# Splitting later weights beside the first MLP: own buffers, and each half chunk requested one step before its split

## Chip, cores, metric

The kernel runs on one core of one Trainium2 chip. The metric is the device time of one execution in microseconds, as the median of several runs. One further execution was taken with the hardware profiler; all rows below are from it.

## The reference

Two transformer layers of width 1024 over 1024 tokens, all in float32. Layer 0 mixes an mLSTM with a block-sparse attention, layer 1 is a sparse latent attention. Behind each mixer stand a LayerNorm, an MLP and a gated per-layer embedding:

```python
h = _layer_norm(DN_ALPHA * h + y, ln1_g[i], ln1_b[i])
u = jnp.square(jax.nn.relu(h @ mlp_w1[i])) @ mlp_w2[i]
h = _layer_norm(DN_ALPHA * h + u, ln2_g[i], ln2_b[i])
h = h + jax.nn.sigmoid(h @ ple_gate_w[i]) * (p[i] @ ple_w[i])
```

`mlp_w1` is 1024 x 4096 and `mlp_w2` 4096 x 1024 for each layer.

## The kernel before, in words

A float32 product is made of three reduced-precision ones: each operand is split into a high part (ScalarE copies it into the reduced type) and a low part (VectorE subtracts the high part), and `mm3` (L159) issues high x high, high x low and low x high, at L164, L167 and L168.

Weights that are used once are loaded into a `wraw` buffer and split there (`wload`, L103; L108 loads, L116 copies, L123 subtracts). Weights of layer 1's mixer that are used later, and more than once or in a hurry, are split ahead of time: `presplit` (L126) takes each [128, up to 1024] weight of `names1` (L884, 22 weights) in half chunks of at most 512 columns, 44 pieces in all. A piece takes two tiles, loads (through L83), copies (L137), subtracts in place (L138) and stores both parts to DRAM (through L86). `presplit` is a generator; `mlp` (L891) takes one step of it after every second output block (L926), in layer 0 alone.

The MLP goes in eight chunks of 512 hidden columns. The first half of a chunk makes the hidden columns: eight PSUM groups of 24 matmuls, each emptied by L907 (ScalarE, relu into a `w2` tile, L906), L908 (VectorE, square) and a split. The second half multiplies them by `mlp_w2`: sixteen PSUM groups of 12 matmuls, each added into H by VectorE (L916 in the first chunk, L918 in later ones). The PSUM tag for both has two banks. The `w2` tag has six buffers in this phase (L261, L482); `presplit` took its tiles from it too.

`tail` (L850) stands before the MLP in the same phase, with the same pools: the output projection with `e_wo`, the residual x loaded into `w2` tiles (L858), summed by L867, LayerNorm (L221) and transposes (L212). Its second half of `e_wo` goes through L116 and L123 as `wu`.

The order on each engine is not written out. A planner (L1652) simulates the program when it is built: each engine takes the instruction that stands earliest in the program among those that are ready and have a buffer, and that order is then fixed, engine by engine. SyncE issues all transfers, in order; an instruction waits for its operands, and whatever stands behind it on its engine waits as well. Buffers of one tag are given out in the order of the program.

Of the kernel before, what the change touches and what calls it, by code (L numbers as in the profile page):

```python
# [8 lines left out]
F32 = mybir.dt.float32  # L9
F32R = mybir.dt.float32r  # L10
BF16 = mybir.dt.bfloat16
I32 = mybir.dt.int32
AF = mybir.ActivationFunctionType
# [4 lines left out]
P = 128  # L18
# [29 lines left out]
class Kern:  # L48
# [77 lines left out]
    def presplit(self, names):  # L126

        nc = self.nc
        for key, src in names:
            n = src.shape[1]  # L130
            self.wd[key] = d = self.dram([P, 2, 1024], F32, "wd")
            for a in range(0, n, 512):
                b = min(a + 512, n)
                lo, hi = (self.w2(dt=F32R)[:, :b - a] for _ in range(2))
                raw = lo.bitcast(F32)
                self.load(raw, src[:, a:b])
                nc.scalar.activation(hi, raw, AF.Copy)  # L137
                nc.vector.tensor_sub(lo, raw, hi.bitcast(F32))  # L138
                self.store(d[:, 0, a:b], hi.bitcast(F32))
                self.store(d[:, 1, a:b], lo.bitcast(F32))  # L140
                yield

    def wget(self, key, n=1024, after=None, into=None):

# [1511 lines left out]
```

## Time and profile before

| | |
|---|---|
| median of three runs | 3027.05 us (3018.58 to 3027.65) |
| the profiled execution | 3019.71 us, span 3018.0 us |
| TensorE busy | 2901.9 us, 96% of the span |
| VectorE, ScalarE busy | 1645.1 us, 1108.4 us |
| granted TensorE clock, mean | 0.987 of full |
| first MLP, second MLP | 719.3 us, 704.5 us |

A row of stages gives, for a stretch of the span, the busy time of each engine with its count of instructions, the granted clock and the DMA engines' share. A row of waits names who waited, for whom, how long in total, how often and the longest. The chain of waits follows the work that ended last back from its end. Both MLPs consist of the same matmuls, so they can be laid side by side.

### The profile page before, as it was taken

To read this page: it belongs to the slowest core of one execution; us is meant where nothing else is said; L and a number is where in the kernel's file an instruction comes from. 1 tells how busy PE (TensorE), PEld (TensorE's weight loads), DVE (VectorE), ACT (ScalarE), POOL (GpSimd) and SP (SyncE) were. 2 spreads that over 40 slices of the span, in tenths; PEclk is the share of its full clock that TensorE was granted. 3 is DMA by queue.
4 is the path that set the end of the run, shared out by engine and by line. 5 is a ranking of instruction groups with operands and counts; after the bars stand their busy time and mean duration, and the time that the engine had idled before them with its cause. 6 is when DMAs were issued, how large, how long until landed. Compare 5 with 4: busy or idle time off the path is not lost.

```text
span 3018.0 us, 39426 instructions
## 1 busy us (share of the span) xinstructions
PE 2901.9 (96%) x14583; PEld 2437.8 (81%) x14583; DVE 1645.1 (55%) x3852; ACT 1108.4 (37%) x2136; POOL 444.8 (15%) x505
## 2 busy tenths in 40 slices
PE   9999999989999999999999897999899999999999
PEld 8888788878787787888887676889788888888887
DVE  3587677765433344334636999975453333333372
ACT  3356654643222222222323668654231111222131
POOL 0254221213000000000412220211120000000032
PEclk9999999999999999999999998999999999999999
DMA  5863544342332334211232347643501111111122
GB/s 198 256 237 121 187 140 152 121 147 101 120 100 87 121 126 139 85 50 49 98 134 79 126 148 252 241 148 131 192 29 56 42 56 42 56 42 56 42 84 84
DMA packets 161552, 352.85 MB, mean 117 GB/s; under 512 B 16976, under 2 KB 68560, under 8 KB 156624
## 3 DMA queue, kind: packets, MB, share of 16 engines
q1 hardware_dynamic: 161360, 350.34, 34.9%
q8 instruction: 115, 1.88, 0.3%
q14 instruction: 77, 0.63, 0.1%
HBM read 242.21 MB, written 108.07 MB: 116 GB/s over the span
## 4 chain that ended last, share of the span: by engine, by line
PE 79%; DVE 9%; DMA 6%; ACT 3%; issue 2%; SPq 0%; POOL 0%; POOLq 0%; ACTq 0%; DVEq 0%
PE psmm L164 21%; PE psmm L167 21%; PE psmm L168 21%; PE psx L823 2%; PE psx L813 2%; PE pss L784 2%; PE psx L212 1%; PE psx L1544 1%; DVE PT L96 1%; PE pss L164 1%; PE pss L167 1%; PE pss L168 1%; DMA qn<-stg 1%; DMA w<-o_wqn 1%; DMA w<-o_wcq 1%
## 5 line engine op out<-in xcount | busy, mean ns | idle before, releaser
L164 PE MATMUL psmm<-wsp,hid 128*128 128x512 f32 x1024 | 400.8, 391 | 12.0 <-DVE H L918 8.0
L168 PE MATMUL psmm<-wsp,hid 128*128 128x512 f32 x1024 | 399.2, 390 | 0.0
L167 PE MATMUL psmm<-h1T,wsp 128*128 128x512 f32 x1024 | 399.0, 390 | 0.2
L167 PE MATMUL psmm<-wsp,hid 128*128 128x512 f32 x1024 | 399.0, 390 | 0.0
L164 PE MATMUL psmm<-h1T,wsp 128*128 128x512 f32 x1024 | 398.2, 390 | 0.6 <-ACT h1T L95 0.6
L168 PE MATMUL psmm<-h1T,wsp 128*128 128x512 f32 x1024 | 398.2, 389 | 0.0
L116 ACT ACTIVATE wsp<-wraw 128x1024 fp32r<-128x1024 f32 (+1 forms) x173 | 182.1, 1053 | 512.2 <-PE psmm L168 477.1
L918 DVE TENSOR_TENSOR H<-psmm,H 128x512 f32<-128x512 f32 x224 | 154.0, 688 | 242.2 <-PE psmm L168 241.6
L908 DVE SCALAR_TENSOR_TENSOR w<-psmm,w 128x512 f32<-128x512 f32 x128 | 88.5, 692 | 340.9 <-ACT w L907 340.9
L123 DVE TENSOR_TENSOR wsp<-wraw,wsp 128x1024 fp32r<-128x1024 f32 (+1 forms) x155 | 192.2, 1240 | 132.6 <-ACT wsp L116 132.0
L201 POOL TENSOR_TENSOR brs<-pw,mhalf 128x1 f32<-128x1 f32 x32 | 25.6, 799 | 1471.3 <-DVE pw L200 1471.3
L164 PEld LDWEIGHTS psmm<-wsp,hid 128*128 128x128 f32 x1024 | 192.6, 188 | 55.5 <-DVE H L918 10.7
L168 PEld LDWEIGHTS psmm<-wsp,hid 128*128 128x128 f32 x1024 | 192.6, 188 | 40.4
L164 PEld LDWEIGHTS psmm<-h1T,wsp 128*128 128x128 f32 x1024 | 192.1, 188 | 40.8 <-ACT h1T L95 1.1
L167 PEld LDWEIGHTS psmm<-h1T,wsp 128*128 128x128 f32 x1024 | 192.2, 188 | 40.2 <-DVE h1T L96 0.8
L167 PEld LDWEIGHTS psmm<-wsp,hid 128*128 128x128 f32 x1024 | 192.7, 188 | 39.4
L168 PEld LDWEIGHTS psmm<-h1T,wsp 128*128 128x128 f32 x1024 | 192.3, 188 | 39.8
L907 ACT ACTIVATE w<-psmm 128x512 f32<-128x512 f32 x128 | 76.6, 598 | 395.4 <-PE psmm L168 395.4
L95 ACT ACTIVATE PT<-psx 128x512 fp32r<-128x512 f32 (+4 forms) x272 | 135.3, 513 | 145.7 <-PE psx L813 77.8
L96 DVE TENSOR_TENSOR PT<-psx,PT 128x512 fp32r<-128x512 f32 (+4 forms) x272 | 154.9, 581 | 59.7 <-ACT PT L95 58.2
L96 DVE TENSOR_TENSOR hid<-w,hid 128x512 fp32r<-128x512 f32 x128 | 88.3, 690 | 64.3 <-ACT hid L95 64.3
L804 POOL TENSOR_SCALAR PP<-PP,nst 128x640 f32<-128x640 f32 (+7 forms) x128 | 97.1, 772 | 91.4 <-DVE nst L847 48.8
(492 smaller groups left out, 6243.4 us busy)
## 6 DMA issues: line engine op xcount, KB each, us to landing
wraw<-mlp_w SPq DMA_DIRECT2D x128, 512.0 KB, 3.6
wsp<-wd SPq DMA_DIRECT2D x36, 1024.0 KB, 6.2
wd<-w SPq DMA_DIRECT2D x80, 256.0 KB, 3.1
wd<-wsp SPq DMA_DIRECT2D x32, 512.0 KB, 3.7
pp<-pst SPq DMA_DIRECT2D x16, 512.0 KB, 2.9
wraw<-ple_gate_w SPq DMA_DIRECT2D x16, 512.0 KB, 3.7
pp<-pp SPq DMA_DIRECT2D x16, 512.0 KB, 4.0
qn<-stg SPq DMA_DIRECT2D x16, 512.0 KB, 3.3
```

Of the source, the lines that this page charges most:

```text
L95: r = nc.scalar.activation(hi, src, AF.Copy)
L96: nc.vector.tensor_sub(lo, src, hi.bitcast(F32))
L116: nc.scalar.activation(sp[0], raw[:, :n], AF.Copy)
L123: nc.vector.tensor_sub(sp[1], raw[:, :n], sp[0].bitcast(F32))
L164: m = nc.tensor.matmul(ps, wh, xh, start=(k == 0), stop=False)
L167: nc.tensor.matmul(ps, wh, xl, start=False, stop=False)
L168: nc.tensor.matmul(ps, wl, xh, start=False, stop=(k == n - 1))
L784: last = nc.tensor.matmul(s[:, :b - a], q[:, hl, pr * 2 + h2, :], K[br - 1][:, a:b], start=(hl == 0), stop=(hl == 1))
L804: nc.gpsimd.tensor_scalar(PP[h2][:, :WT], PP[h2][:, :WT], st[:, 3, h2:h2 + 1], 1.0, op0=ALU.mult, op1=ALU.mult)
L907: nc.scalar.activation(r, ps, AF.Relu)
L908: nc.vector.scalar_tensor_tensor(out=r, in0=ps, scalar=0.0, in1=r, op0=ALU.max, op1=ALU.mult)
L918: nc.vector.tensor_add(hs, ps, hs)
```

## The change

`presplit` becomes two loops. An inner generator takes the pieces in order, makes their two tiles from a tag of its own, `pre`, with four buffers of [128, 512], and requests the load. The outer loop requests the first piece at the first step; at each later step it requests the next piece and then splits and stores the one requested a step earlier. The 44 pieces now take 45 steps (of 56 that the MLP's first seven chunks offer). Copy, subtraction and stores are the same.

```diff
-        for key, src in names:
-            n = src.shape[1]
-            self.wd[key] = d = self.dram([P, 2, 1024], F32, "wd")
-            for a in range(0, n, 512):
-                b = min(a + 512, n)
-                lo, hi = (self.w2(dt=F32R)[:, :b - a] for _ in range(2))
-                raw = lo.bitcast(F32)
-                self.load(raw, src[:, a:b])
-                nc.scalar.activation(hi, raw, AF.Copy)
-                nc.vector.tensor_sub(lo, raw, hi.bitcast(F32))
-                self.store(d[:, 0, a:b], hi.bitcast(F32))
-                self.store(d[:, 1, a:b], lo.bitcast(F32))
-                yield
+        def land():
+            for key, src in names:
+                n = src.shape[1]
+                self.wd[key] = d = self.dram([P, 2, 1024], F32, "wd")
+                for a in range(0, n, 512):
+                    b = min(a + 512, n)
+                    lo, hi = (self.sm([P, 512], F32R, tag="pre", bufs=4)[:, :b - a] for _ in range(2))
+                    self.load(lo.bitcast(F32), src[:, a:b])
+                    yield d[:, :, a:b], lo, hi
+
+
+        pieces = land()
+        ahead = next(pieces, None)
+        while ahead is not None:
+            yield
+            now, ahead = ahead, next(pieces, None)
+            d, lo, hi = now
+            nc.scalar.activation(hi, lo.bitcast(F32), AF.Copy)
+            nc.vector.tensor_sub(lo, lo.bitcast(F32), hi.bitcast(F32))
+            self.store(d[:, 0], hi.bitcast(F32))
+            self.store(d[:, 1], lo.bitcast(F32))
```

## Rows read from the trace of the kernel before

**Rows 1.** The page: busy us, share of the span, instructions of each engine
```profile
PE 2901.9 (96%) x14583; PEld 2437.8 (81%) x14583; DVE 1645.1 (55%) x3852; ACT 1108.4 (37%) x2136; POOL 444.8 (15%) x505
```

**Rows 2.** Stages, both MLPs whole: stretch, us, busy by engine, clock, DMA share
```profile
747.50:1466.80 719.30, 707.57 (x3130) 582.82 (x3129) 305.61 (x425) 185.41 (x260) 20.73 (x15) 1.00 0.29 93
2215.70:2920.20 704.50, 703.45 (x3130) 582.37 (x3128) 279.44 (x381) 159.51 (x216) 20.81 (x15) 1.00 0.15 48
```

**Rows 3.** Stages by chunk: first, third, fourth, sixth of one MLP; first, second of the other
```profile
747.50:841.60 94.10, 91.14 (x412) 74.42 (x411) 40.66 (x61) 26.06 (x41) 3.29 (x3) 1.00 0.31 97
...
931.20:1023.30 92.10, 89.26 (x386) 73.08 (x385) 36.29 (x49) 22.70 (x32) 0.00 (x0) 0.98 0.36 114
1023.30:1111.40 88.10, 87.38 (x386) 72.01 (x385) 36.21 (x49) 22.72 (x32) 0.00 (x0) 1.00 0.36 120
...
1200.90:1288.40 87.50, 87.31 (x385) 71.99 (x384) 33.69 (x45) 20.41 (x28) 0.00 (x0) 1.00 0.26 85
...
2215.70:2306.60 90.90, 90.50 (x411) 74.56 (x409) 36.55 (x52) 22.02 (x33) 3.32 (x3) 1.00 0.15 47
2306.60:2393.70 87.10, 87.10 (x386) 72.12 (x385) 31.33 (x41) 17.88 (x24) 0.00 (x0) 1.00 0.16 49
```

**Rows 4.** Waits of TensorE in the first MLP: total us, times, longest
```profile
PE psmm L164 <- DVE H L918: 8.0, 5, 2.7
PE psmm L164 <- DVE H L916: 2.6, 2, 1.9
```

**Rows 5.** Waits of ScalarE and VectorE in the first MLP
```profile
ACT w L137 <- DMA w<-o_wkv: 17.1, 8, 4.4
...
ACT w L137 <- DMA w<-o_wuk: 6.1, 3, 2.3
...
DVE w L138 <- ACT w L137: 62.6, 39, 4.0
```

**Rows 6.** Chain of waits in the second chunk: start us, us, what
```profile
885.32 3.86 DMA w<-o_wcq
...
889.27 0.64 ACT w L137
...
889.93 0.70 DVE w L138
...
890.65 0.33 SPq L86
...
891.02 3.81 DMA w<-o_wcq
```

**Rows 7.** Timeline, second chunk, VectorE and TensorE: start us, us, engine, line, what
```profile
907.93 0.69 DVE L138 TENSOR_TENSOR w<-w,w 128x512 fp32r<-128x512 f32 x1 [2.53 <-ACT w L137]
908.54 0.68 DVE L918 TENSOR_TENSOR H<-psmm,H 128x512 f32<-128x512 f32 x1
...
909.28 0.50 PE L164 MATMUL psmm<-wsp,hid 128*128 128x512 f32 x1 [2.24 <-DVE H L918]
```

**Rows 8.** Two lines (ns min/median/max, first and last start us); a row of SyncE's timeline
```profile
L411 POOL TENSOR_SCALAR an<-an x1: 1508/1508/1508, 21.3 to 21.3; 128x512 f32<-128x512 f32 x1
...
L500 ACT ACTIVATE mg<-mg x1: 311/311/311, 118.6 to 118.6; 32x128 f32<-32x128 f32 x1
...
675.51 0.43 SPq L83 DMA_DIRECT2D row<-ln_g  x1
```

**Rows 9.** DMA issues from 795 to 1262 us: count, KB each, median us to landing
```profile
wd<-w SPq DMA_DIRECT2D x80, 256.0 KB, 3.1
w<-o_wcq SPq DMA_DIRECT2D x8, 256.0 KB, 3.8
```

**Rows 10.** Layer 0's projection: a stage (columns as rows 2), a wait of TensorE
```profile
671.80:690.00 18.20, 15.55 (x60) 12.04 (x59) 11.23 (x15) 4.57 (x5) 0.00 (x0) 0.91 0.82 276
...
PE psmm L164 <- ACT wu L116: 0.5, 1, 0.5
```

## Prediction

> **What bounds the kernel now.** I read the busy table first. TensorE is busy 96% of the span [rows 1], so the time can only change where TensorE stands idle or runs at its lower clock, and the question is how much of that belongs to the split of the later weights. The kernel holds its own control: the second MLP does the same matmuls as the first with the same code, but has no such split beside it. So I next cut both MLPs out by stage. The first takes 719.3 us, the second 704.5 us, with the same 3130 matmuls [rows 2]. The 14.8 us between them is the price of the split as it stands and the most that the change can win inside this stage. Chunk by chunk it lies where the pieces are: the first chunk costs 94.1 against 90.9 us, the third 92.1 against about 87.1, the sixth, with only four pieces left, 87.5 [rows 3]. About half a per cent of the kernel is at stake.
>
> Then the waits. In the first MLP TensorE waits 8.0 us for L918 and 2.6 us for L916 on VectorE [rows 4], the two lines that empty a PSUM bank. These lines are not slow; they are late, because VectorE runs in order and L138 stands ahead of them. ScalarE's L137 waits for its own load in eight rows of the table, 17.1 us for the first weight down to 6.1 us for the last, 89.6 us when all eight are added, and L138 waits 62.6 us for L137 [rows 5]. The chain of waits shows the loop: load 3.86 us, copy 0.64, subtraction 0.70, store issued, and only behind that store, on the same in-order queue, the load of the next but one piece at 891.02, 5.70 us after 885.32 [rows 6]. At the end of the chunk's eight pieces L138 starts at 907.93, L918 behind it at 908.54, and TensorE has stood for 2.24 us at 909.28 [rows 7]. The 10.6 us of waits and 14.8 us differ by a slow restart after each stop: at the one in the third chunk the granted clock is 0.98 of full over the chunk, 1.00 in its neighbours [rows 3].
>
> **The change part by part.** *Own buffers.* Two 128x512 tiles a piece came from the six w2 buffers that the relu results (L906) use too; now four buffers hold two pieces and nothing else. No instruction is added or taken away: 44 copies, 44 subtractions, 44 loads, 88 stores as before. What changes is what holds a piece back. In before, a piece's buffer follows the relu tiles ahead of it in w2, so eight pieces run in a bunch once the eight relu tiles of a chunk have been given out; the bunch of the second chunk starts at 885.32, right where its second half starts. After it, a piece waits for nothing but the pieces before it.
>
> *Where the pieces then go.* The planner takes an instruction as soon as its engine is free and its buffer is there, however late it stands in the program: L411 stands behind L500 in the program, and runs at 21.3 us, L500 at 118.6; and the ln1 row asked for at mb 6 is loaded at 675.51, among the first x loads [rows 8]. The pool of the four buffers opens with that of the x loads, at about 672 us. So I expect the first loads of the split at about 677 us, not at 795, and the whole split ahead of its place in the program: beside the output projection of layer 0 and the first chunk of the MLP. `yield` gives a place in the program, not a time.
>
> *Pace.* With two pieces in flight, a load must wait until a store of the piece two before has landed. One turn is a load of 3.8 us, a copy of 0.64 and a store of 3.1 [rows 6, 9], 7.5 us for two pieces, 3.8 for one; 44 take 167 us, from 677 to about 844, the end of the first chunk. Chunks two to six then have no piece beside them.
>
> *Gain.* The 14.8 us go from their present place [rows 2]. *Cost one, in the projection.* From 671.8 to 690.0 the DMA engines are 82% busy at 276 GB/s [rows 10], so full is some 337 GB/s and 256 KB take 0.78 us (an estimate from that row). TensorE already waits 0.5 us there for the second half of the e_wo weights [rows 10]. Two loads and two stores of the split may come ahead of those weights, 4 x 0.78 = 3.1 us, and nothing covers that, since TensorE already waits. Bounds: 0 if the weights stay ahead on SyncE's queue; about 3.1 + 3.8 = 6.9 if a store that waits for its piece's load also holds their issue back [rows 9]. I take 3.1. *Cost two, lateness.* A matmul's share of the second MLP is 704.5 / 3130 = 0.225 us [rows 2]. Beside the projection and the first half of a chunk a PSUM bank lasts 24 matmuls, 5.4 us, beside the second half 12, 2.7 us. With two banks and 0.7 us to empty one [rows 7], VectorE may be about 4.7 us late in the one and 2.0 in the other before TensorE stops. The bunch of [rows 7] used up those 2.0 us and cost 2.24 more in eight pieces: (2.0 + 2.24) / 8 = 0.53 us of lateness a piece. I let the pieces up to 795 us be covered by the longer banks, and charge the 13 that remain beside the second half of the first chunk: 13 x 0.53 - 2.0 = 4.9 us. Bounds: 0, if the thinner traffic brings the loads in time; 44 x 0.53 - 2.0 = 21.3, if lateness adds up over all pieces. VectorE has room for the 0.7 us of a piece in the projection: the layer's LayerNorm is there too, and its place (cost one) is where a surplus would show. I take 4.9, the value of the stage most like [rows 7].
>
> *Sum.* 14.8 - 3.1 - 4.9 = 6.8 us less. The profiled execution took 3019.7 us, which gives 3012.9; the median of the runs shown is 3027.05, 7.3 above it, which gives 3020.2. The runs lie near both levels, so I give the middle, 3017.
>
> *A rule beside the rows.* The Trainium skill, "DMA: Bandwidth & Descriptors", section "Rules for kernel authors", says to issue a transfer early, compute, and wait on its semaphore late, so that the fixed cost overlaps. By that rule the change wins all of its 14.8 us, which is the second case below. The rows agree in part only: loads in [rows 6] were already requested while the piece before was being split, and were waited for all the same, since landing took longer than the split.
>
> **The rivals.** *Every wait is covered* (chance 0.26). Step ahead of need, buffers without the relu tiles, traffic thinner than in the bunches: the loads land before ScalarE comes to them. For: outside the bunch nothing in [rows 4] stops TensorE. Against: the loop of [rows 6] stays, with one pair fewer. Time: 14.8 less, 3004.9 on the profiled execution, 3012 on the median's level. It also takes in the case that pieces keep to their places, one in two PSUM groups, with a request 5.4 us ahead of a 3.8 us landing.
>
> *Lateness adds up* (chance 0.22, slower). The mechanism is one: in-order ScalarE and VectorE with copies planned for loads that land sooner than they do. Bunches of eight end, and VectorE catches up: the chunk after the bunch has no wait. A chain of 44 has no such pause, and two pieces in flight tie every load to a store's landing, 3.1 us that a third pair covered. Price: 21.3 + 3.1 - 14.8 = 9.6 us more, 3029.3 on the profiled execution, 3036.6 on the median's level. It decides from (14.8 - 3.1 + 2.0) / 44 = 0.31 us of lateness a piece. For it: the 0.53 of [rows 7]. Against: that was with three pairs' transfers in flight at a time, not two, and a PSUM bank lasts twice as long up to 795 us.
>
> *It does not do what it says* (chance 0.10). Loads are requested early already; if planned order keeps every split right behind its load, the same stops come in other places, and the time stays within 2 us of 3019.7 or 3027.
>
> **How the numbers follow.** The forecast, 6.8 us less with 2 to 11 as its own range (3009 to 3024 over both levels), has 0.42. About 0.3% of the time, 9.1 us, is what a measurement can tell from no change. The forecast reaches that with a third of its weight (0.13), the covered case nearly always (0.24): faster 0.37. Slower: the adding-up case in most of its weight, plus a little of the rest, 0.20. Same: 0.43. The range takes the covered case down to 3005 and the slower one up to 3034, which leaves about 1 in 10 out on either side.
>
> **What would show it.** Right: the first load of the split near 677 us, the last copy before 860; chunks two to six at 87.1 us each; L138 no longer ahead of L918 there; a longer wait of TensorE for the e_wo weights near 688 us and some waits for L916 in the first chunk. Wrong: loads that still start at 795 and at each chunk's second half (the pool did not free them); a projection that is 6 us or more longer (cost one too small); waits of TensorE for L867, L907 or L908 before 795 us (the longer banks did not cover); a first chunk well above 100 us (lateness adds up).

## The result, and the profile after

The changed kernel takes 3045.87 us (median of five runs, 3043.36 to 3058.26), the kernel before 3022.95 us beside it: 1.0081 of the time before, 95% interval [1.0064, 1.0098], some 24 us slower. Forecast was 3017, range 3005 to 3034. The profiled execution of the changed kernel has a span of 3044.1 us, 26.1 more than that of before.

In the listing of the changed kernel lines have moved: the load of a piece is still issued through L83 and its stores through L86, the copy is L146, the subtraction L147; L875, L916, L924 and L926 are what L867, L908, L916 and L918 were, and L172 is the first matmul of a product.

First the stages: stretch, us, busy time of TensorE, its weight loads, VectorE, ScalarE and GpSimd, granted clock, DMA share, GB/s. The projection of layer 0 in the kernel before, for which no row stands above:

```profile
671.80:747.50 75.70, 73.05 (x334) 60.06 (x333) 44.59 (x75) 21.82 (x25) 21.82 (x14) 0.98 0.37 125
```

and in the changed kernel the projection, the first MLP whole, and its first two chunks [rows 2, 3]:

```profile
676.96:771.18 94.22, 75.36 (x335) 60.90 (x333) 55.97 (x93) 32.15 (x44) 22.17 (x14) 0.93 0.77 249
771.18:1492.36 721.18, 710.54 (x3128) 585.08 (x3129) 295.76 (x407) 173.72 (x240) 20.41 (x14) 0.99 0.23 74
771.18:878.70 107.52, 97.52 (x408) 77.24 (x409) 52.80 (x79) 36.22 (x57) 2.93 (x2) 0.95 0.68 218
878.70:965.80 87.10, 87.10 (x386) 72.12 (x385) 31.30 (x41) 17.89 (x24) 0.00 (x0) 1.00 0.16 49
```

From the second chunk on the MLP is clean, 87.1 us a chunk. The price has moved ahead and grown: 94.2 - 75.7 = 18.5 us in the projection, 721.2 - 704.5 = 16.7 us in the first MLP, all of it in the first chunk (107.5 against the 90.9 of the second MLP's first chunk). That is 35.2 us, where the kernel before paid 14.8: 20.4 of the 26.1 us. The other 5.2 stand ahead of the projection, which starts at 676.96 and not at 671.8; on every engine the instructions up to there stand in the same order in both programs, and in the traces of the twelve experiments below too, where the projection starts anywhere from 669.1 to 678.3 us. So this is variation between executions.

What the planner did with the pieces is seen on SyncE (start us, us, engine, line, what):

```profile
680.92 0.43 SPq L83 DMA_DIRECT2D row<-ln_g  x1
...
682.61 1.41 SPq L83 DMA_DIRECT2D pre<-o_wkv  x2
...
688.25 0.33 SPq L83 DMA_DIRECT2D pre<-o_wkv  x1
...
690.64 1.05 SPq L86 DMA_DIRECT2D wd<-pre  x2
```

The split begins beside the projection, right behind the LayerNorm rows, 113 us ahead of where it began before. Three loads are out before the first store: three of the four buffers are taken by loaded tiles, and one is left for a high part. The waits of ScalarE and VectorE from 677 to 879 us (total us, times, longest) show what follows:

```profile
ACT pre L146 <- DMA wd<-pre: 81.6, 35, 4.9
...
DVE pre L147 <- ACT pre L146: 62.3, 38, 3.3
```

In [rows 5] the copy waited for its load; now it waits 81.6 us for a store, and VectorE waits behind it as long as before (62.6 us then). The chain of waits (start us, us, what) tells which store:

```profile
739.12 3.15 DMA wd<-pre
...
742.37 0.64 ACT pre L146
743.03 3.60 DMA wd<-pre
...
746.74 0.64 ACT pre L146
747.40 3.29 DMA wd<-pre
...
750.76 0.64 ACT pre L146
751.39 0.02 issue
751.42 0.69 DVE pre L147
752.11 0.61 DVE H L875
```

Each copy follows the landing of the store of the piece just before it, some 4 us a turn, and the turn is unbroken. Whatever stands behind the subtraction on VectorE is late with it. On the timelines of VectorE and TensorE:

```profile
752.03 0.68 DVE L875 SCALAR_TENSOR_TENSOR H<-w,psmm 128x512 f32<-128x512 f32 x1
...
752.76 0.79 PE L172 MATMUL psmm<-wu,yT 128*128 128x512 f32 x1 [5.56 <-DVE H L875]
```

TensorE's waits from 677 to 879 us (compare [rows 4]) are 28.6 us in all, of which these six rows hold 28.0:

```profile
PE psmm L172 <- DVE H L875: 8.4, 3, 5.6
PE psmm L172 <- DVE w L916: 7.5, 3, 3.6
PE psmm L172 <- ACT h1T L95: 6.0, 2, 5.7
PE psmm L172 <- ACT wu L116: 2.7, 1, 2.7
PE psx L220 <- DVE pw L208: 1.7, 1, 1.7
PE psmm L172 <- DVE H L924: 1.7, 3, 0.8
```

They are spread over several kinds of work that VectorE and ScalarE do for TensorE, PSUM and transposes alike. Against the projection of before and the second MLP, TensorE's idle time in the two stages grew by 25.8 us and its busy time for the same work by 9.4, which makes up the 35.2. The second part goes with the clock: the granted clock is 0.93 of full in the projection and 0.95 in the first chunk.

### The profile page after: what moved, and what is told of

Same layout as the page of the kernel before. It is cut to its first block, busy times and chain, and to the rows that moved or that the text cites. A ratio compares the mean times of both kernels' runs of the same rounds, so it can differ in the third digit from the quotient of the medians.

```text
span 3044.1 us, 39369 instructions
## 1 busy us (share of the span) xinstructions
PE 2914.5 (96%) x14583; PEld 2446.0 (80%) x14583; DVE 1642.4 (54%) x3852; ACT 1107.3 (36%) x2136; POOL 444.6 (15%) x505
## 4 chain that ended last, share of the span: by engine, by line
PE 78%; DVE 9%; DMA 7%; ACT 3%; issue 3%; SPq 0%; POOL 0%; ACTq 0%; POOLq 0%; DVEq 0%
PE psmm L172 21%; PE psmm L175 21%; PE psmm L176 21%; DMA wd<-pre 4%; PE psx L831 2%; PE pss L792 2%; PE psx L821 2%; PE psx L220 1%; DVE PT L96 1%; PE psx L1552 1%; ACT pre L146 1%; PE pss L172 1%; DMA qn<-stg 1%; PE pss L175 1%; PE pss L176 1%
## 5 line engine op out<-in xcount | busy, mean ns | idle before, releaser
L172 PE MATMUL psmm<-h1T,wsp 128*128 128x512 f32 x1024 | 399.6, 391 | 9.2 <-ACT h1T L95 6.3
L172 PE MATMUL psmm<-wsp,hid 128*128 128x512 f32 x1024 | 400.6, 391 | 7.7 <-DVE w L916 4.6
L926 DVE TENSOR_TENSOR H<-psmm,H 128x512 f32<-128x512 f32 x224 | 154.4, 689 | 296.6 <-PE psmm L176 296.5
L123 DVE TENSOR_TENSOR wsp<-wraw,wsp 128x1024 fp32r<-128x1024 f32 (+1 forms) x155 | 191.9, 1239 | 136.8 <-ACT wsp L116 136.2
L916 DVE SCALAR_TENSOR_TENSOR w<-psmm,w 128x512 f32<-128x512 f32 x128 | 88.5, 692 | 321.3 <-ACT w L915 321.3
L172 PEld LDWEIGHTS psmm<-h1T,wsp 128*128 128x128 f32 x1024 | 192.8, 188 | 50.5 <-ACT h1T L95 7.2
L172 PEld LDWEIGHTS psmm<-wsp,hid 128*128 128x128 f32 x1024 | 192.6, 188 | 50.5 <-DVE w L916 5.4
```

The source lines that it names most:

```text
L123: nc.vector.tensor_sub(sp[1], raw[:, :n], sp[0].bitcast(F32))
L172: m = nc.tensor.matmul(ps, wh, xh, start=(k == 0), stop=False)
L916: nc.vector.scalar_tensor_tensor(out=r, in0=ps, scalar=0.0, in1=r, op0=ALU.max, op1=ALU.mult)
L926: nc.vector.tensor_add(hs, ps, hs)
```

## The experiments

Two theories stood against each other at first. **P** (plan): the pieces run as early as their buffers let them, each copy placed right behind the transfer that it needs, and the in-order engines are late at each. **B** (buffers): the copy's wait for the store is what costs. **D**, beside them: the traffic of the split. All times are ratios to the kernel before, with 95% intervals; the stages are from one profiled execution each, and "price" is what projection and first MLP take over 75.7 and 704.5 us together. The second MLP, which no change touches, is the same within 0.1 us in all fourteen traces; the projection, where no piece stands beside it, takes 75.0 to 76.2 us. So prices that differ by less than about 1 us are not told apart.

| kernel | of the time before | projection, us | first MLP, us | price, us |
|---|---|---|---|---|
| before | 1 | 75.7 | 719.3 | 14.8 |
| changed | 1.0081 [1.0064, 1.0098] | 94.2 | 721.2 | 35.2 |
| hi_apart | 1.0079 [1.0064, 1.0095] | 92.9 | 726.5 | 39.2 |
| start_gate | 1.0057 [1.0037, 1.0077] | 75.6 | 736.3 | 31.7 |
| bunch8 | 1.0034 [1.0020, 1.0048] | 75.0 | 727.1 | 21.9 |
| half_free | 1.0016 [1.0001, 1.0031] | 93.4 | 707.5 | 20.7 |
| six | 0.9992 [0.9980, 1.0003] | 85.9 | 710.5 | 16.2 |
| pool_start | 0.9994 [0.9978, 1.0009] | 75.4 | 718.5 | 13.7 |
| gated_w2 | 0.9965 [0.9953, 0.9976] | 75.6 | 708.4 | 3.8 |
| gated_own | 0.9935 [0.9915, 0.9955] | 75.8 | 707.2 | 2.8 |
| dma_only | 0.9931 [0.9908, 0.9954] | 76.7 | 704.6 | 1.1 |
| gated | 0.9943 [0.9928, 0.9958] | 76.2 | 704.5 | 0.5 |
| pool_queue | 0.9949 [0.9934, 0.9963] | 75.6 | 705.0 | 0.4 |
| gated_load | 0.9941 [0.9918, 0.9965] | 75.8 | 704.5 | 0.1 |

**hi_apart: two tags.**

```diff
-lo, hi = (self.sm([P, 512], F32R, tag="pre", bufs=4)[:, :b - a] for _ in range(2))
+lo, hi = (self.sm([P, 512], F32R, tag=t, bufs=2)[:, :b - a] for t in ("pre", "prh"))
```

> The changed kernel with two tags of two buffers in place of one of four: one for the loaded tiles, one for the high parts. In the changed kernel the copies on ScalarE wait 81.6 us for a store of the piece before to land, because the loads that run ahead hold three of the four buffers. Theory B (buffers: that wait is what costs): the wait on stores falls below 20 us, TensorE's waits in the projection of layer 0 and the first chunk shrink, and the time falls to the kernel before or under it, 0 to 14 us less. Theory P (plan: pieces are taken as early as buffers allow and each copy is placed right behind the transfer that it needs, so in-order ScalarE and VectorE stop at every piece): the copies wait for loads or for older stores instead, the 44 pieces stand closer together, and the time stays 10 to 30 us above the kernel before.

The copies wait for loads now, 95 us in eight rows of which this is the longest, and none waits for a store:

```profile
ACT prh L146 <- DMA pre<-o_wqn: 22.7, 7, 7.2
```

The price is 39.2 us. As P had it: the name of the wait changed, the price did not go. B in the form "the wait for the store costs" falls here.

**gated: the pieces back at their places.** `mm3` keeps its last matmul; the edges give the planner an order and make no wait on the chip.

```diff
-self.load(lo.bitcast(F32), src[:, a:b])
+self.load(lo.bitcast(F32), src[:, a:b], self.lastmm)
...
-nc.scalar.activation(hi, lo.bitcast(F32), AF.Copy)
+self.order(nc.scalar.activation(hi, lo.bitcast(F32), AF.Copy), self.lastmm)
```

> The changed kernel with its four buffers, but each load is ordered behind the last matmul of the output block at its step, and each copy behind that of its own step, by an order edge for the planner alone (no wait on the chip). So the pieces go back to their places in the program, one in two PSUM groups (5.4 us). Theory P: no pieces beside the projection, a load has a whole step to land, TensorE does not stop at them, the first MLP takes 705 to 709 us; 8 to 15 us less than the kernel before. Theory B: the four buffers are shared as before, the copies still wait for the store of the piece before; the step hides part of it, 0 to 8 us less. Theory D (the traffic of the split is what costs): within 4 us of the kernel before.

3006.1 us, 0.9943 of before: all of the 14.8 us are gone from the first MLP, which takes what the second takes. Its stage, ScalarE's waits for stores, and all waits of TensorE in the first MLP:

```profile
747.09:1451.58 704.49, 703.50 (x3130) 582.22 (x3129) 304.86 (x425) 185.30 (x260) 20.73 (x15) 1.00 0.30 95
...
ACT pre L146 <- DMA wd<-pre: 103.8, 30, 5.6
...
PE psmm L172 <- DVE pw L208: 0.6, 1, 0.6
PE psmm L172 <- ACT h1T L95: 0.3, 1, 0.3
```

ScalarE waits longer for stores than in the changed kernel, 103.8 against 81.6 us, and it costs nothing: the wait ends before anything behind it is due. So it is the place, not the wait.

**gated_w2, gated_own, gated_load: what the parts of the change bring once the place is right.** gated_w2 is the kernel before with the edge on the load; gated_own adds the four own buffers; gated_load is the changed kernel with the edge on the load alone.

```diff
 # gated_w2 and gated_own: the kernel before
-self.load(raw, src[:, a:b])
+self.load(raw, src[:, a:b], self.lastmm)
 # gated_own as well
-lo, hi = (self.w2(dt=F32R)[:, :b - a] for _ in range(2))
+lo, hi = (self.sm([P, 512], F32R, tag="pre", bufs=4)[:, :b - a] for _ in range(2))
 # gated_load: the changed kernel
-self.load(lo.bitcast(F32), src[:, a:b])
+self.load(lo.bitcast(F32), src[:, a:b], self.lastmm)
```

> The kernel before, with its shared w2 buffers and its load right ahead of its split, and only each load ordered behind the last matmul of the output block at its step. It tells own buffers and the step ahead from the place alone. Theory P: the bunches of eight are gone, each copy is still placed right behind its load, so ScalarE waits some 2 to 3 us at each, but a pause follows every piece and the two PSUM banks catch it: first MLP 705 to 712 us, 5 to 13 us less than the kernel before. Theory B: no store is waited for here, the load still is, 0 to 4 us less. If this is as fast as the gated kernel with own buffers, own buffers and the early request bring nothing of their own.

> The kernel before with the four own buffers, the load still right ahead of its split (no step ahead), and each load ordered behind the output block of its step. Against gated_w2 (708.4 us for the first MLP; shared w2 buffers) it tells the own buffers alone, against gated_load (704.5 us) the request a step ahead alone. Theory P: the place is the main thing, 704.5 to 708.5 us either way; if own buffers are what is left, 704.5 to 705.5; if the early request is, 707 to 708.5.

> The gated kernel without the order edges on the copies: own buffers and the request a step ahead, loads ordered behind their output blocks, copies placed where the planner has them. It tells what the edge on the copy brings beside gated (704.5 us for the first MLP) and, beside gated_w2 (708.4 us, w2 buffers, load right ahead of its split), what own buffers bring once the place is right. Theory P: copies are placed right behind their loads or right behind the store whose buffer they take, but a pause follows each piece: 704.5 to 708.5 us for the first MLP, 11 to 16 us less than the kernel before.

In the first MLP the place alone takes 719.3 to 708.4 us, 10.9 of 14.8; own buffers take 1.2 more, to 707.2; the request a step ahead the last 2.7, to 704.5. Both ideas of the change bring something once the place is held, 3.9 us together, and little beside the place itself. The edge on the copy adds nothing (704.5 with and without). The intervals of the three whole times overlap, so between them only the stages decide, in one execution of each.

**dma_only: transfers without the split.** Copy and subtraction are left out, both parts are stored as loaded.

```diff
-nc.scalar.activation(hi, lo.bitcast(F32), AF.Copy)
-nc.vector.tensor_sub(lo, lo.bitcast(F32), hi.bitcast(F32))
-self.store(d[:, 0], hi.bitcast(F32))
+self.store(d[:, 0], lo.bitcast(F32))
```

> The changed kernel without the copy and the subtraction of the split: both parts are stored as loaded, so the split of these weights is left out, and the matmuls of layer 1 that use them get the raw values twice. Loads and stores of the split stay, as early as the planner takes them; ScalarE and VectorE have nothing of it. Theory P and B: the price is paid on the in-order engines, so it goes: 8 to 15 us less than the kernel before, with only the wait for the e_wo weights (2.7 us in the changed kernel) left in the projection. Theory D (traffic): the projection of layer 0 stays 10 us or more longer than in the kernel before, and the time 5 us or more above it.

The projection, with all of the split's traffic beside it:

```profile
669.08:745.81 76.73, 73.02 (x334) 60.11 (x333) 44.07 (x75) 21.82 (x25) 21.79 (x14) 0.98 0.98 341
```

The DMA engines are 98% busy at 341 GB/s, more than in the changed kernel (0.77, 249), and the projection is 1.0 us longer than before. D falls. The whole kernel came out 21 us below before (14 to 28 by the interval), where 8 to 15 were expected; these two stages hold 13.7 of it.

**start_gate: the chain moved out of the projection.** The edge is on the two loads of the first weight alone (the condition is shortened here).

```diff
-self.load(lo.bitcast(F32), src[:, a:b])
+self.load(lo.bitcast(F32), src[:, a:b], self.lastmm if ... key == ("wkv", 0) else None)
```

> The changed kernel, with one order edge for the planner: the first load stands behind the first output block of the MLP's first chunk. From there all 44 pieces run as early as their buffers let them, beside the MLP's first chunks and not beside the projection. The changed kernel lost, against stretches without pieces, 18.5 us in the projection of layer 0 and 16.7 us in the first MLP, 0.80 us a piece over 44. Theory P (every piece of an unbroken chain makes in-order engines later, wherever it stands): the projection is back at 75 to 77 us, the first MLP takes 730 to 740 us, the kernel 10 to 20 us more than before. Rival L (the place is wrong: VectorE is full of LayerNorm beside the projection): the first MLP takes 710 to 722 us, within 9 us of the kernel before.

The projection is back at 75.6 us, and the first MLP pays 31.8. The place beside LayerNorm is not worse than another; the chain brings its price along.

**half_free and bunch8: shorter chains.** In half_free the first 22 pieces are free and the rest have the edges of gated; in bunch8 each eight pieces hang on the block at which the first of them is requested.

```diff
 # half_free
+self.npc += 1
-self.load(lo.bitcast(F32), src[:, a:b])
+self.load(lo.bitcast(F32), src[:, a:b], self.lastmm if self.npc > 22 else None)
 # bunch8
+self.bgate = self.lastmm if self.npc % 8 == 0 else self.bgate
+self.npc += 1
-self.load(lo.bitcast(F32), src[:, a:b])
+self.load(lo.bitcast(F32), src[:, a:b], self.bgate)
```

> The changed kernel with its first 22 pieces as early as their buffers let them, beside the projection, and the other 22 with load and copy ordered behind the output blocks of their steps as in the gated kernel, which stood at 704.5 us for the first MLP. Theory P: the price is by the piece of the unbroken chain; the projection is as long as in the changed kernel, 90 to 94 us, the first chunk of the MLP and all later ones cost nothing, and the kernel takes 0 to 5 us more than the kernel before (18.5 - 14.8). Rival S (a start-up cost: the first loads beside x and e_wo do it, not the number of pieces): the time is near the changed kernel, 15 us or more above the kernel before. Rival L: as P.

> The changed kernel with the loads of each eight pieces ordered behind the output block at which the first of the eight is requested: chains of eight with a pause behind each, in the second half of chunks one to six, with own buffers. It tells the length of the chain: 44 pieces in one chain cost 35.2 us (0.80 a piece), 22 cost 20.7 us. Theory P: lateness adds up only within a chain, and the 2 us that two PSUM banks allow are free in each; 8 x 0.8 - 2.0 = 4.4 us a chunk, 20 to 26 us over 5.5 chunks, the first MLP 722 to 732 us. If the pause matters more than that (VectorE catches up inside the chain), 708 to 720 us, as the kernel before (719.3).

22 free pieces cost 20.7 us, 0.94 a piece; 44 in bunches of eight 21.9 us, 0.50 a piece, which fits P, where each bunch has the room of its two PSUM banks for nothing; 44 in a row 35.2 us, 0.80 a piece. In half_free 3.0 us of it fell into the first chunk, where nothing was expected.

**pool_start and pool_queue: the same chain on an engine that empties no PSUM.** pool_start is start_gate with copy and subtraction on GpSimd; in pool_queue GpSimd issues the pieces' loads and stores as well.

```diff
 # pool_start
-nc.scalar.activation(hi, lo.bitcast(F32), AF.Copy)
-nc.vector.tensor_sub(lo, lo.bitcast(F32), hi.bitcast(F32))
+nc.gpsimd.tensor_copy(hi, lo.bitcast(F32))
+nc.gpsimd.tensor_sub(lo, lo.bitcast(F32), hi.bitcast(F32))
 # pool_queue as well
-self.store(d[:, 0], hi.bitcast(F32))
-self.store(d[:, 1], lo.bitcast(F32))
+nc.gpsimd.dma_start(d[:, 0], hi.bitcast(F32))
+nc.gpsimd.dma_start(d[:, 1], lo.bitcast(F32))
```

> The start_gate kernel with copy and subtraction of the split on GpSimd, which has nothing to do in the MLP's chunks. The same unbroken chain of loads and stores with the same four buffers, the same waits, but on an engine that empties no PSUM bank. Theory P (the price is what stands behind a late piece on ScalarE and VectorE): the first MLP takes 704 to 706 us, the kernel 12 to 17 us less than before, though GpSimd waits for loads or stores at most of its pieces. Theory B (the wait itself) or D (traffic): the first MLP stays 5 us or more above 704.5.

> The pool_start kernel, where the split ran on GpSimd and the first MLP still took 718.5 us, because SyncE issues the MLP's weight loads in order behind stores that waited for GpSimd (ScalarE waited 66.9 us for mlp_w weights). Here GpSimd also issues the loads and stores of the split. Theory P: with neither ScalarE, VectorE nor SyncE behind a late piece, the first MLP takes 704 to 706 us, and the kernel 12 to 17 us less than before. Theory B or D (the waits or the traffic as such): 5 us or more above 704.5, as in pool_start.

pool_start missed: 718.5 us in place of 704 to 706. ScalarE's wait for MLP weights in the first MLP, SyncE's wait for the copies on GpSimd before it could issue their stores, and SyncE at 1000 us:

```profile
ACT wsp L116 <- DMA wraw<-mlp_w: 62.1, 8, 23.1
...
SPq L86 <- POOL pre L146: 29.3, 13, 4.0
...
1000.39 0.43 SPq L86 DMA_DIRECT2D wd<-pre  x1
1000.92 0.36 SPq L108 DMA_DIRECT2D wraw<-mlp_w  x1
```

SyncE is in order too: the weight load at L108 stood behind stores that waited for a late GpSimd, ScalarE waited for it up to 23.1 us at a time, and the lateness went round by the weights. With the pieces' transfers on GpSimd it is gone, though GpSimd waits for stores all along:

```profile
750.40:1455.43 705.03, 703.94 (x3131) 582.10 (x3129) 290.27 (x381) 159.67 (x216) 175.28 (x235) 1.00 0.29 95
...
POOL pre L146 <- DMA wd<-pre: 84.6, 43, 3.9
```

The same unbroken chain with the same four buffers costs 0.4 us there. It also runs slower: from the first to the last subtraction it takes 260 us, where start_gate takes 164 and pool_start 210. Slower transfers are not what saves it, since dma_only ran them denser for 1.1 us. The price is what stands in order behind a late piece, on ScalarE, VectorE and SyncE.

**six: three pieces in flight.**

```diff
-tag="pre", bufs=4
+tag="pre", bufs=6
```

> The changed kernel with six buffers in its tag, three pieces, as many as w2 has. Theory P: pieces run ahead just the same, in a chain of 44 that the planner packs closer; in-order engines are late at every piece; the projection and the first MLP together stay 25 to 40 us above their stretches without pieces (35.2 in the changed kernel), the kernel 10 to 25 us above before. Rival N (four buffers were too few): copies find a buffer without waiting for a store, and the time falls to within 5 us of the kernel before or under it.

P missed here, and the rival's time holds. Projection, first MLP, and ScalarE's waits for stores:

```profile
669.21:755.10 85.89, 73.50 (x335) 60.01 (x333) 61.47 (x99) 33.94 (x47) 20.68 (x14) 0.96 0.92 304
755.10:1465.62 710.52, 706.92 (x3128) 584.28 (x3128) 292.63 (x401) 171.39 (x237) 22.27 (x15) 1.00 0.22 71
...
ACT pre L146 <- DMA wd<-pre: 23.4, 13, 2.9
```

The price is 16.2 us, less than half of that with four buffers. So P as it was put, that a free chain costs what it costs whatever its buffers, is too strong. That the lateness of a piece is what a turn takes longer on the chip than in the plan, and that buffers set this, would fit; it is not shown, since the plan's own times stand in no trace.

How late a piece is can be read by holding the changed kernel against gated, where nothing stops TensorE: nearly the same VectorE instructions, in nearly the same order, stand around the pieces in both. In gated, VectorE's fourth L875 of the projection and its eighth L924 of the first chunk:

```profile
679.34 0.68 DVE L875 SCALAR_TENSOR_TENSOR H<-w,pss 128x512 f32<-128x512 f32 x1
...
817.33 0.68 DVE L924 SCALAR_TENSOR_TENSOR H<-H,psmm 128x512 f32<-128x512 f32 x1
```

In the changed kernel the first subtraction stands behind that L875 and two LayerNorm statistics (L234), and the last one behind that L924, another subtraction and one L123:

```profile
690.65 0.69 DVE L147 TENSOR_TENSOR pre<-pre,pre 128x512 fp32r<-128x512 f32 x1 [3.18 <-ACT pre L146]
...
857.41 0.68 DVE L924 SCALAR_TENSOR_TENSOR H<-H,psmm 128x512 f32<-128x512 f32 x1
...
860.91 0.69 DVE L147 TENSOR_TENSOR pre<-pre,pre 128x512 fp32r<-128x512 f32 x1 [0.54 <-ACT pre L146]
```

The plan put the pieces into a stretch that lasts 138.0 us where nothing stops; they took 170.3. If the plan counted on about the times of gated, that is 32.3 us over 43 turns, 3.96 us a turn on the chip for 3.21 in the plan, 0.75 us of lateness each. It is the price of 35.2 us read once more, on VectorE, and no second proof of it. The same reading gives 153.4 and 190.2 us for hi_apart (36.8; price 39.2), 126.0 and 163.7 for start_gate (37.7; price 31.7), 120.8 and 133.6 for six (12.8; price 16.2).

## Why the prediction was wrong

**What bounded the kernel: right.** The 14.8 us were the most to win, and gated, gated_load and pool_queue win them.

**Where the pieces go: right.** The first load was forecast near 677 us and came at 682.61, in an execution that was 5.2 us late by then; the last copy was forecast before 860 and came at 860.25; chunks two to six were forecast at 87.1 us and take 87.0 to 87.1.

**Pace: right in size, for another reason.** 3.8 us a piece were forecast, 3.96 measured. But the loads were not in the loop: three of four buffers were held by loads that ran ahead, and the copy waited for the store of the piece just before, one store and 0.64 us of copy a turn. That the fourth buffer would go to a third load was not seen.

**Cost one: not confirmed.** It was put at 3.1 us for the e_wo weights, and TensorE's wait for them grew from 0.5 to 2.7 us. But that wait goes from nothing to 2.1 us in kernels without a piece beside the projection (bunch8, gated_load), is 1.0 us in half_free, which has pieces there, and is missing in dma_only, which has the most traffic. The 2.2 us can be chance.

**Cost two, lateness, is the step that failed.** It was put at 4.9 us, and about 33 (35.2 - 2.2) were paid. Its main error is that the pieces beside the projection and the first half of a chunk were taken as covered, because a PSUM bank lasts 5.4 us there. The first chunk by halves, in the second MLP and then in the changed kernel (columns as above), and the first half of the second chunk in start_gate:

```profile
2215.70:2263.10 47.40, 47.00 (x219) 38.51 (x217) 21.56 (x32) 16.77 (x27) 3.32 (x3) 1.00 0.14 45
2263.10:2306.60 43.50, 43.50 (x193) 36.05 (x192) 14.99 (x20) 5.25 (x6) 0.00 (x0) 1.00 0.16 49
...
771.18:826.57 55.39, 50.85 (x216) 40.50 (x217) 29.65 (x46) 23.39 (x40) 2.93 (x2) 0.94 0.74 242
826.57:878.70 52.13, 46.66 (x192) 36.75 (x193) 23.15 (x33) 12.83 (x18) 0.00 (x0) 0.97 0.62 193
...
846.67:902.70 56.03, 47.00 (x193) 36.68 (x193) 23.29 (x32) 19.82 (x32) 0.00 (x0) 0.97 0.75 234
```

The projection paid 18.5 us and the first half 8.0, where cost two had nothing; the second half, where it had 4.9, paid 8.6. In start_gate a first half, with the same longer banks and no LayerNorm beside it, took 56.0 us for the 43.5 that it takes without pieces. A slack is used up once: lateness of 0.75 us a piece fills 4.7 us in six pieces.

The second error is the size of the term, 0.53 us a piece. Its working divided by eight pieces, but the stop came at the seventh; the eighth subtraction of the chunk stands behind it in the kernel before:

```profile
910.88 0.68 DVE L138 TENSOR_TENSOR w<-w,w 128x512 fp32r<-128x512 f32 x1
```

With seven it is 0.61. And it came from a tag with six buffers: bunch8, with four, paid 21.9 / 5.5 = 4.0 us a chunk, which by the same working is (2.0 + 4.0) / 8 = 0.75 us. The upper bound of the step, all pieces added up, was the right sum with too small a term: 44 x 0.75 - 2.0 = 31 us is near the 33 of the changed kernel and the 31.7 of start_gate. It is an estimate and not exact: for the 22 free pieces of half_free it gives 14.5, and 20.7 were paid.

Of the signs of being wrong that the prediction lists, three came: the longer projection, waits of TensorE for what were L867 and L908 (8.4 and 7.5 us), and a first chunk above 100 us.

**The rivals.** The slower one, lateness that adds up over an unbroken chain, is what happened; it had 0.22 and a price of 9.6 us more, where 20.4 us more were measured in the two stages. Its limit of 0.31 us a piece for breaking even was not tested by itself, since a piece's lateness is read from the price; six, with a price of 16.2 us against 14.8, came out even with the kernel before.

The Trainium skill ("DMA: Bandwidth & Descriptors", "Rules for kernel authors") says to issue early and wait late. The runs agree where the order held the pieces at their places: the request a step ahead brought 2.7 us there (gated_own to gated_load). Where nothing held them, as in the changed kernel, the early request came with a price of 35.2 us.

**What stays open.** Whether a turn is shorter in the plan than on the chip, and why, is not shown: the plan's own times stand in no trace. A store in the changed kernel's stretch lands after a median of 3.3 us; whether the plan has this, or the queueing ahead of it, shorter was not tried.

## What to carry to other kernels

Under a planner that takes work as soon as it has a buffer, own buffers remove an order as well as a wait: before giving background work its own tag, ask what its old buffers held back, and tie it to its place with an order edge instead. Background work on engines that also empty PSUM should come in pieces with a pause behind each (here a step of 5.4 us, for stores that land in 3.1 [rows 9]); slack is spent once, lateness adds up by the piece. A wait in a profile is not yet a cost: 103.8 us of waits for stores cost nothing where the next thing due was further away.

## What the runs showed of the hardware

A projection stage ran beside DMA engines that were 98% busy at 341 GB/s and took 1.0 us longer than beside 37% at 125 GB/s: traffic alone did not hurt the transfers that TensorE waited for. An in-order issue queue carries lateness between engines: 13.7 us came back through SyncE after the split had left ScalarE and VectorE, and 0.4 were left when GpSimd issued its own transfers. Work on GpSimd made VectorE's longer: with the split on GpSimd in pool_queue, the 381 VectorE instructions of the first MLP were busy for 290.3 us, in the second MLP [rows 2] for 279.4; it cost no time there, and why it is so was not tried. And stops cost more than their length: in the projection of the changed kernel, with 94.22 - 75.36 = 18.9 us in which TensorE stood still, the granted clock fell to 0.93 of full, and its busy time for the same matmuls rose from 73.05 to 75.36 us.
